# Gates by column reduction and a DRAM round trip instead of a row accumulation and ones products, with a fourth transpose bank

## The chip, the core and the metric

The kernel runs on one core of a Trainium2 chip. The metric is device time in microseconds from start to end of one execution. Five engines run their own instruction streams: TensorE (PE, whose weight loads the profile lists as PEld), VectorE (DVE), ScalarE (ACT), GpSimd (POOL) and SyncE (SP, which here only issues transfers). PSUM, the memory that PE writes, is used as eight tiles (banks) of 128 x 512 fp32.

## What is computed

A decoder trunk of two layers over 256 tokens of width 1024. Each layer is a feed-forward half step, a token mixer (block attention in the first layer, latent attention in the second) and another feed-forward half step. Every sub-layer has a shift, a scale and a gate computed from the conditioning vector `c`:

```
c_act = silu(c)
for layer in range(2):
    mods = c_act @ ada_w[layer] + ada_b[layer]
    sh1, sc1, g1, sh2, sc2, g2, sh3, sc3, g3 = split(mods, 9)
    h = modulate(rms_norm(x, norm_g[layer, 0]), sh1, sc1)
    x = x + 0.5 * g1 * swiglu(h, w_gate, w_up, w_down)
    h = modulate(rms_norm(x, norm_g[layer, 1]), sh2, sc2)
    x = x + g2 * (moba_attention(h) if layer == 0 else mla_attention(h))
    h = modulate(rms_norm(x, norm_g[layer, 2]), sh3, sc3)
    x = x + 0.5 * g3 * swiglu(h, w_gate, w_up, w_down)
```

Each of the six gates is a vector of 1024, the product of `c_act` with a 1024 x 1024 matrix.

## The kernel before

Tokens lie in two tiles of 128 partitions. Weights come from DRAM through SP into three buffers `raw` (`wload`, L787), and `split` (L677 to L682) makes two parts of each 128 x 1024 piece: `hi` by a copy on ScalarE (L680), `lo` by a subtraction on DVE (L681). There are eight buffers of each. A product of near full precision is then three matmuls of such parts (`mm3`, L810 to L812), or two matmuls in the gate and up products of the feed-forward (L1017, L1025). Attention scores (L1097 in the first layer) and value products (L1152) use full fp32.

The modulation matrices stream in parallel, 512 KB a tile of 128 x 1024, through three buffers `adaw` (`ada_tile`, L705 to L708), and are worked off on DVE between the weights' subtractions. There are two ways:

- **Shift and scale** (`column`, L688 to L692). The matrix is stored transposed, so that a partition holds one output's row. One DVE instruction multiplies the tile by `c_b`, `silu(c)` in all partitions, sums along the row and adds the bias; a small instruction (`DVE_READ_ACCUMULATOR2`) writes the sum. The outcome is a column: one value a partition.
- **Gate** (`ada_gate`, L721 to L745). A gate multiplies values whose 1024 columns lie along the free axis (`resid`, L920), so it is needed as a row in all partitions. The matrix is stored untransposed; eight DVE instructions (L729) add tile times `c` into `acc` (128 x 1024, set to zero and given the bias row by GpSimd, L727 and L728). Then `acc` is split, and `sums` adds its 128 partitions by four matmuls with a matrix of ones, two to each half of 512 columns (L739, L740), in the tile `adaps` of a PSUM bank kept for it (`ps_ada`). ScalarE copies the result, halved for feed-forward gates, into the gate tile (L742). There are two gate buffers.

The eight PSUM banks are four for products (`ps_mm`), three for transposes and attention (`ps_tr`) and that one.

The order of instructions on each engine is worked out on the host at build time by the class `Order`. It has each instruction's dependencies and an estimated length, and places instructions by need time on five engines, with buffers, banks and transfers in flight as limits (`place`). PE instructions of gate sums have a rule of their own: they are first in line (-1, L468 and L469) but are taken only after standing ready for `GATE_MARGIN` (L435), or when nothing else is there. After four rounds, `work_out` tries variations of the need times from the seeds in `TRIALS` and keeps each that ends earlier by its own estimate. Any change in the program therefore gives another order on every engine.

Of the kernel before, what the change touches and what calls it, by code (L numbers as in the profile page):

```python
# [22 lines left out]
P = 128  # L23
# [107 lines left out]
def lay_out(v):  # L131
# [13 lines left out]
    out["first"] = np.concatenate([first[:, :, :FIRST_A].reshape(KD, -1), first[:, :, FIRST_A:].reshape(KD, -1)], axis=1)  # L145
    mats, cols, rows = [], np.zeros((P, 3, NK), np.float32), []
    for key, i in vectors():
        w, b, c = ((v["kv_ada_w"], v["kv_ada_b"], i) if key == "kv" else
                   (v["ada_w"][key[0]], v["ada_b"][key[0]], 3 * key[1] + i))
        w, b = w[:, c * D:(c + 1) * D], b[c * D:(c + 1) * D]  # L150
        mats.append((w if i == 2 else w.T).reshape(KD, P, D))
        if i == 2:
            rows.append(b)
        else:
            c0 = NORMS.index(key) * KD
            cols[:, i, c0:c0 + KD] = b.reshape(KD, P).T
# [7 lines left out]
    for g in (v["mla_q_g"][0], v["mla_k_g"]):  # L164
        more += [np.concatenate([g[:DH], np.ones(P - DH, np.float32)])[:, None], np.tile(g[None, DH:], (P, 1))]
    out.update(ada=np.stack(mats), rows=np.stack(rows), cols=np.concatenate([cols.reshape(P, -1), *more], axis=1))

# [10 lines left out]
def bcast_row(ap, n, parts=P):  # L178
# [17 lines left out]
MARGIN = 400.0  # L196
GATE_MARGIN = 3000.0
ROUND_OF_ORDER = 4

TRIALS = (6, 9, 17, 64, 78, 124, 144, 157, 188, 238, 252, 394, 434, 436, 447, 579, 698, 701, 758, 764, 1127,  # L200
          1232, 1334, 1357, 1411, 1493, 1778, 1903)
ENGINES = ("PE", "DVE", "Activation", "Pool", "SP")
# [55 lines left out]
class Order:  # L258
# [128 lines left out]
    def place(self, need):  # L387
# [43 lines left out]
        def choose(e, t):  # L431
            av = avail[e]
            if e == "PE":
                first = min(av)
                old = [x for x in av if x[2] <= t - (GATE_MARGIN if x[0] < 0 else MARGIN)]  # L435
                x = min(old) if old else min(av, key=lambda x: (x[0] < 0, x))
                if x is not first and first[2] <= t and order[e] and order[e][-1] in self.pre[first[1]]:
                    x = first
                return x
# [16 lines left out]
        while placed < n:  # L456
# [9 lines left out]
            while known[e] and known[e][0][0] <= t:  # L466
                r, k = heapq.heappop(known[e])
                first = e == "PE" and any(u.startswith("adaps") for u in self.tiles_of[k])  # L468
                avail[e].append((-1 if first else need[k], k, r))  # L469
            x = choose(e, t)  # L470
# [104 lines left out]
def trunk(ctx: ExitStack, tc: tile.TileContext, a: dict, out: bass.AP):  # L575
# [10 lines left out]
    ps_mm = ctx.enter_context(tc.tile_pool(name="ps_mm", bufs=4, space=PSUM))  # L586
    ps_tr = ctx.enter_context(tc.tile_pool(name="ps_tr", bufs=3, space=PSUM))
    ps_ada = ctx.enter_context(tc.tile_pool(name="ps_ada", bufs=1, space=PSUM))

    uid = [0]  # L590

    def nm(s):
        uid[0] += 1
        return f"{s}_{uid[0]}"
# [57 lines left out]
    make_identity(nc, ident)  # L652
    ones_r = cp.tile([P, P], F32R, name="ones_r")
    ones = ones_r.bitcast(F32)
    nc.vector.memset(ones, 1.0)
    ident_b = cp.tile([P, P], BF16, name="ident_b")
# [14 lines left out]
    cols, cact = all_cols[:, :3 * NK].rearrange("p (i c) -> p i c", i=3), places["c"]  # L671
    m_cols = cp.tile([P, 2, NK], F32, name="m_cols")

    c_b = cp.tile([P, D], F32, name="c_b")
# [46 lines left out]
    def ada_gate(j, key, row):  # L721

        for k in range(KD):
            with noted(late if key == (1, 2) else set()):
                if k == 0:
                    acc = adap.tile([P, D], F32, tag="acc", name=nm("acc"), bufs=1)
                    nc.gpsimd.memset(acc, 0.0)  # L727
                    nc.gpsimd.dma_start(acc[0:1, :], a["rows"][row:row + 1, :])  # L728
                nc.vector.scalar_tensor_tensor(acc, ada_tile(j, k), cact[:, k:k + 1], acc, op0=ALU.mult, op1=ALU.add)  # L729
            if k < KD - 1:  # L730
                yield
        ahi, alo = split(acc, D)
        t = mods[key, "g"] = modp.tile([P, D], F32, tag="gate", name=nm("gate"))

        def sums():
            for hh in range(2):
                pt = ps_ada.tile([P, 512], F32, tag="ada", name=nm("adaps"))
                sl = slice(hh * 512, (hh + 1) * 512)
                nc.tensor.matmul(pt, ones_r, ahi[:, sl], start=True, stop=False)  # L739
                nc.tensor.matmul(pt, ones_r, alo[:, sl], start=False, stop=True)  # L740
                pe(0.44)
                nc.scalar.activation(t[:, sl], pt, AF.Copy, scale=1.0 if key[1] == 1 else 0.5)  # L742
            ready.add((key, "g"))
        later(3.0, sums)
        yield  # L745
# [72 lines left out]
    def tr_tile():  # L818
        return ps_tr.tile([P, 512], F32, tag="tr", name=nm("tr"))
# [747 lines left out]
    def first(units):  # L1567
# [5 lines left out]
        with ExitStack() as st:  # L1573
# [51 lines left out]
            hold(lambda: nc.scalar.activation(cact, cact, AF.Silu), 10e3)  # L1625
            ps_x = [tr_tile(), ps_ada.tile([P, 512], F32, tag="ada", name=nm("tr"))]
            accs = [tr_tile() if f >= 4 else mm_tile() for f in range(B1)]
# [119 lines left out]
```

## Time and profile before

| | |
|---|---|
| runs before | 991.25, 991.40 and 991.53 us; median 991.4 us |
| profiled execution | span 989.0 us from the first to the last instruction; its own whole time isn't listed apart, and the median of the runs is 2.4 us above its span |
| granted PE clock, mean | 0.996 |
| bytes read from and written to DRAM | 255.37 MB and 4.19 MB |

The profile has a page (busy time by engine, the chain of work that ended last, groups of equal instructions, transfers) and further views of the same trace: waits by who ended them, busy time in chosen windows, the instructions of one tile, and a timeline. In a row such as "L739 PE MATMUL adaps<-hi,ones_r 128*128 128x512 f32 x12 | 4.7, 394 | 0.0", L739 is the line of the kernel, then come engine, operation, what is written and read, shapes and how many; then busy us, mean ns of one, and idle time of the engine just before them with what ended it. Matmuls overlap in the pipeline, so their lengths add up to more than the time that they take.

The program's stages, by the profile's order of time: the first feed-forward until about 210 us, block attention until about 330, feed-forwards until about 515 and about 700, latent attention until about 800, and the last feed-forward.

### The profile page before, as it was taken

To read this page: it belongs to the slowest core of one execution; us is meant where nothing else is said; L and a number is where in the kernel's file an instruction comes from. 1 tells how busy PE (TensorE), PEld (TensorE's weight loads), DVE (VectorE), ACT (ScalarE), POOL (GpSimd) and SP (SyncE) were. 2 spreads that over 40 slices of the span, in tenths; PEclk is the share of its full clock that TensorE was granted. 3 is DMA by queue.
4 is the path that set the end of the run, shared out by engine and by line. 5 is a ranking of instruction groups with operands and counts; after the bars stand their busy time and mean duration, and the time that the engine had idled before them with its cause. 6 is when DMAs were issued, how large, how long until landed. Compare 5 with 4: busy or idle time off the path is not lost.

```text
span 989.0 us, 15277 instructions
## 1 busy us (share of the span) xinstructions
PE 978.4 (99%) x5583; PEld 832.5 (84%) x5583; DVE 845.8 (86%) x1433; ACT 631.5 (64%) x1180; POOL 83.8 (8%) x120
## 2 busy tenths in 40 slices
PE   8999999999999999999999999999999999999998
PEld 6988888878877888888888888888888888888887
DVE  7999999898998999999799999984899889677542
ACT  5689565378756966655367666643879796667421
POOL 1012010022230000000000000000142110000000
PEclk8999999999999999999999999999999999999999
DMA  9978989898777778988989988883343468545630
GB/s 368 408 253 286 338 301 360 307 346 316 261 291 232 246 281 321 334 317 300 366 294 344 339 308 310 291 301 109 107 155 119 179 233 302 191 171 173 229 131 22
DMA packets 53419, 260.57 MB, mean 263 GB/s; under 512 B 6208, under 2 KB 7008, under 8 KB 35168
## 3 DMA queue, kind: packets, MB, share of 16 engines
q1 hardware_dynamic: 51840, 255.93, 71.2%
q0 software_dynamic: 1024, 3.17, 1.1%
q8 instruction: 44, 0.72, 0.3%
q10 hardware_dynamic: 480, 0.49, 0.2%
q14 instruction: 31, 0.25, 0.1%
HBM read 255.37 MB, written 4.19 MB: 262 GB/s over the span
## 4 chain that ended last, share of the span: by engine, by line
PE 86%; issue 9%; DVE 3%; ACT 1%; POOL 1%; DMA 1%; SPq 0%; DVEq 0%; ACTq 0%; POOLq 0%
PE mm L1017 24%; PE mm L810 13%; PE mm L812 13%; PE mm L811 13%; PE mm L1025 12%; PE at L1152 1%; PE at L1132 1%; PE tr L1253 1%; PE at L1092 1%; PE tr L860 1%; PE tr L1524 1%; DVE lo L681 1%; PE at L1097 1%; PE mm L1694 1%; PE mm L1693 1%
## 5 line engine op out<-in xcount | busy, mean ns | idle before, releaser
L681 DVE TENSOR_TENSOR lo<-raw,hi 128x1024 fp32r<-128x1024 f32 (+3 forms) x312 | 369.4, 1199 | 66.7 <-ACT hi L680 61.3
L680 ACT ACTIVATE hi<-raw 128x1024 fp32r<-128x1024 f32 (+3 forms) x312 | 321.0, 1041 | 151.8 <-PE mm L812 114.5
L1017 PE MATMUL mm<-h,hi 128*128 128x512 f32 x1120 | 289.0, 394 | 0.0
L1017 PEld LDWEIGHTS mm<-h,hi 128*128 128x128 f32 x1120 | 199.6, 189 | 34.7 <-DVE g L955 0.3
L1025 PEld LDWEIGHTS mm<-h,lo 128*128 128x128 f32 x1120 | 155.7, 190 | 12.2
L1025 PE MATMUL mm<-h,lo 128*128 128x256 f32 x1120 | 162.5, 282 | 0.0
L691 DVE CUSTOM_DVE_ANT_0 adaw<-adaw,c_b,cols 128x1024 f32<-128x1024 f32 x112 | 142.0, 1280 | 3.7 <-ACT c_b L1624 1.9
L810 PE MATMUL mm<-hi,gh 128*128 128x512 f32 (+1 forms) x356 | 137.0, 388 | 0.0
L811 PE MATMUL mm<-lo,gh 128*128 128x512 f32 (+1 forms) x356 | 136.8, 387 | 0.0
L812 PE MATMUL mm<-hi,gl 128*128 128x512 f32 (+1 forms) x356 | 136.8, 387 | 0.0
L810 PE MATMUL mm<-hi,h 128*128 128x512 f32 (+1 forms) x240 | 93.7, 399 | 0.2
L811 PE MATMUL mm<-lo,h 128*128 128x512 f32 (+1 forms) x240 | 92.8, 392 | 0.0
L812 PE MATMUL mm<-hi,h 128*128 128x512 f32 (+1 forms) x240 | 91.9, 392 | 0.5 <-DVE h L826 0.4
L812 PEld LDWEIGHTS mm<-hi,gl 128*128 128x128 f32 x356 | 66.9, 188 | 13.6
L810 PEld LDWEIGHTS mm<-hi,gh 128*128 128x128 f32 x356 | 66.9, 188 | 13.4
L811 PEld LDWEIGHTS mm<-lo,gh 128*128 128x128 f32 x356 | 66.9, 188 | 13.2
L729 DVE SCALAR_TENSOR_TENSOR acc<-adaw,cols,acc 128x1024 f32<-128x1024 f32 x48 | 61.8, 1288 | 0.4 <-DMA adaw<-in_ada_dram 0.2
L810 PEld LDWEIGHTS mm<-hi,h 128*128 128x128 f32 x240 | 44.9, 188 | 10.0 <-issue 1.3
L812 PEld LDWEIGHTS mm<-hi,h 128*128 128x128 f32 x240 | 44.9, 188 | 9.7 <-DVE h L826 1.2
L811 PEld LDWEIGHTS mm<-lo,h 128*128 128x128 f32 x240 | 45.0, 188 | 7.9 <-issue 0.2
L954 ACT ACTIVATE u<-mm 128x256 f32<-128x256 f32 x70 | 26.4, 377 | 35.6 <-PE mm L1025 34.5
L847 POOL TENSOR_TENSOR rstd<-ssq,mhalf 128x1 f32<-128x1 f32 x12 | 13.7, 1139 | 411.3 <-DVE ssq L842 369.0
(241 smaller groups left out, 1257.3 us busy)
## 6 DMA issues: line engine op xcount, KB each, us to landing
raw<-in_w_dram SPq DMA_DIRECT2D x142, 1024.0 KB, 5.3
adaw<-in_ada_dram SPq DMA_DIRECT2D x160, 512.0 KB, 5.5
raw<-in_w_dram SPq DMA_DIRECT2D x12, 512.0 KB, 3.5
raw<-in_first_dram SPq DMA_DIRECT2D x7, 512.0 KB, 9.0
raw<-in_w_dram SPq DMA_DIRECT2D x6, 576.0 KB, 3.8
bias_d<-bt SPq DMA_DIRECT2D x12, 256.0 KB, 4.0
bg<-bias_d POOLq DMA_DIRECT2D x4, 768.0 KB, 7.7
raw<-in_first_dram SPq DMA_DIRECT2D x10, 256.0 KB, 8.7
```

The lines of the kernel that those rows point to most:

```text
L680: nc.scalar.activation(hi, src, AF.Copy)
L681: nc.vector.tensor_tensor(lo, src, hi.bitcast(F32), op=ALU.subtract)
L691: nc.vector.tensor_tensor_reduce(wt, wt, c_b, 1.0, cols[:, i, c:c + 1], op0=ALU.mult, op1=ALU.add, accum_out=m_cols[:, i, c:c + 1])
L729: nc.vector.scalar_tensor_tensor(acc, ada_tile(j, k), cact[:, k:k + 1], acc, op0=ALU.mult, op1=ALU.add)
L810: nc.tensor.matmul(ps, lh, rh, start=start, stop=False)
L811: nc.tensor.matmul(ps, lh, rl, start=False, stop=False)
L812: nc.tensor.matmul(ps, ll, rh, start=False, stop=stop)
L847: nc.gpsimd.tensor_tensor(r, stats[t], mhalf[:, 0:1], op=ALU.pow)
L860: nc.tensor.transpose(kslice(pt, j), kslice(y, j), ident)
L954: nc.scalar.activation(x, ps[:, S:], AF.Copy)
L1017: nc.tensor.matmul(ps[i], w[0], hs[2], start=k == 0, stop=False)
L1025: nc.tensor.matmul(ps[i][:, S:], w, hk_, start=False, stop=k == KD - 1)
```

## The change

- The gate's matrix is laid out transposed too, with output `8 p + k` in partition `p` of tile `k`, and the gate's eight tiles go through the same DVE instruction as shift and scale. The biases of all gates are one table `gates` of 128 x 48, loaded once into `g_cols`; each gate's eight columns there are its sums' starting values and are overwritten by the sums.
- For the four feed-forward gates a DVE instruction halves the eight columns.
- SP writes the 128 x 8 columns to a DRAM buffer of 1024 values, in which they stand as a row, and reads the row back into all 128 partitions as the gate tile.
- `acc`, its memset and bias load, its split, the matmuls with ones, the ScalarE copies, `ones_r` and the rule on gate sums in `Order` are gone. The bank of `ps_ada` goes to `ps_tr`, which has four. `TRIALS` has other seeds.

```
@@ lay_out
-        mats.append((w if i == 2 else w.T).reshape(KD, P, D))
+        mats.append(w.T.reshape(P, KD, D).transpose(1, 0, 2) if i == 2 else w.T.reshape(KD, P, D))
         if i == 2:
-            rows.append(b)
+            gates.append(b.reshape(P, KD))
...
@@ Order
-GATE_MARGIN = 3000.0
...
-                old = [x for x in av if x[2] <= t - (GATE_MARGIN if x[0] < 0 else MARGIN)]
-                x = min(old) if old else min(av, key=lambda x: (x[0] < 0, x))
+                old = [x for x in av if x[2] <= t - MARGIN]
+                x = min(old or av)
...
@@ trunk
-    ps_tr = ctx.enter_context(tc.tile_pool(name="ps_tr", bufs=3, space=PSUM))
-    ps_ada = ctx.enter_context(tc.tile_pool(name="ps_ada", bufs=1, space=PSUM))
+    ps_tr = ctx.enter_context(tc.tile_pool(name="ps_tr", bufs=4, space=PSUM))
...
+    g_cols = cp.tile([P, 6 * KD], F32, name="g_cols")
+    gate_d = [dp.tile([D], F32, name=f"gate_d{i}") for i in range(6)]
...
@@ ada_gate
+        if not row:
+            hold(lambda: nc.sync.dma_start(g_cols, a["gates"]))
+        g = g_cols[:, row * KD:(row + 1) * KD]
         for k in range(KD):
             with noted(late if key == (1, 2) else set()):
-                if k == 0:
-                    acc = adap.tile([P, D], F32, tag="acc", name=nm("acc"), bufs=1)
-                    nc.gpsimd.memset(acc, 0.0)
-                    nc.gpsimd.dma_start(acc[0:1, :], a["rows"][row:row + 1, :])
-                nc.vector.scalar_tensor_tensor(acc, ada_tile(j, k), cact[:, k:k + 1], acc, op0=ALU.mult, op1=ALU.add)
+                wt = ada_tile(j, k)
+                nc.vector.tensor_tensor_reduce(wt, wt, c_b, 1.0, g[:, k:k + 1], op0=ALU.mult, op1=ALU.add,
+                                               accum_out=g[:, k:k + 1])
...
-        ahi, alo = split(acc, D)
+        if key[1] != 1:
+            nc.vector.tensor_scalar(g, g, 0.5, None, op0=ALU.mult)
+        nc.sync.dma_start(gate_d[row].rearrange("(p k) -> p k", k=KD), g)
         t = mods[key, "g"] = modp.tile([P, D], F32, tag="gate", name=nm("gate"))
-
-        def sums():
-            for hh in range(2):
-                pt = ps_ada.tile([P, 512], F32, tag="ada", name=nm("adaps"))
-                sl = slice(hh * 512, (hh + 1) * 512)
-                nc.tensor.matmul(pt, ones_r, ahi[:, sl], start=True, stop=False)
-                nc.tensor.matmul(pt, ones_r, alo[:, sl], start=False, stop=True)
-                pe(0.44)
-                nc.scalar.activation(t[:, sl], pt, AF.Copy, scale=1.0 if key[1] == 1 else 0.5)
-            ready.add((key, "g"))
-        later(3.0, sums)
+        nc.sync.dma_start(t, bcast_row(gate_d[row], D))
+        ready.add((key, "g"))
         yield
```

Three places show how the order moves. The first is PE in block attention, at the scores of the last of four head groups. `at` and `mm` tiles written from `kT,qT` are scores (L1097 before, L1086 after); `mm` tiles written from `hi` or `lo` and `oT` are the output projection. Before:

```order
L1097 MATMUL at_3722<-kT_3691,qT_3690 128x128
L1097 MATMUL mm_3723<-kT_3691,qT_3690 128x128
L1097 MATMUL at_3724<-kT_3691,qT_3690 128x256
L810 MATMUL mm_3623<-hi_3494,oT 128x512
L811 MATMUL mm_3623<-lo_3495,oT 128x512
L812 MATMUL mm_3623<-hi_3494,oT 128x512
L810 MATMUL mm_3623<-hi_3494,oT 128x512
L811 MATMUL mm_3623<-lo_3495,oT 128x512
L810 MATMUL mm_3622<-hi_3650,oT 128x512
L1097 MATMUL at_3725<-kT_3691,qT_3690 128x256
L1097 MATMUL at_3724<-kT_3691,qT_3690 128x256
L1097 MATMUL at_3725<-kT_3691,qT_3690 128x256
```

After:

```order
L1086 MATMUL at_3700<-kT_3669,qT_3668 128x128
L1086 MATMUL mm_3701<-kT_3669,qT_3668 128x128
L1086 MATMUL at_3702<-kT_3669,qT_3668 128x256
L1086 MATMUL at_3703<-kT_3669,qT_3668 128x256
L1086 MATMUL at_3702<-kT_3669,qT_3668 128x256
L1086 MATMUL at_3703<-kT_3669,qT_3668 128x256
L799 MATMUL mm_3601<-hi_3472,oT 128x512
```

Before, six projection matmuls stand between the wide scores (128 x 256); after, the wide scores are one block.

The second is PE a little later, at the value products of the same group: `at` written from `pT,v` (L1152 before, L1141 after). Before:

```order
L1152 MATMUL at_3820<-pT_3804,v_3261 64x128 x2
L1152 MATMUL at_3820<-pT_3811,v_3261 64x128 x2
L810 MATMUL mm_3624<-hi_3785,oT 128x512
L811 MATMUL mm_3624<-lo_3786,oT 128x512
L812 MATMUL mm_3624<-hi_3785,oT 128x512
L811 MATMUL mm_3625<-lo_3629,oT 128x512
L810 MATMUL mm_3623<-hi_3650,oT 128x512
L1152 MATMUL at_3820<-pT_3818,v_3261 64x128 x2
L1152 MATMUL at_3820<-pT_3804,v_3261 64x128 x2
L1152 MATMUL at_3820<-pT_3811,v_3261 64x128 x2
L1152 MATMUL at_3820<-pT_3818,v_3261 64x128 x2
```

After:

```order
L799 MATMUL mm_3601<-hi_3628,oT 128x512
L1141 MATMUL at_3798<-pT_3782,v_3239 64x128 x2
L1141 MATMUL at_3798<-pT_3789,v_3239 64x128 x2
L1141 MATMUL at_3798<-pT_3796,v_3239 64x128 x2
L1141 MATMUL at_3798<-pT_3782,v_3239 64x128 x2
L1141 MATMUL at_3798<-pT_3789,v_3239 64x128 x2
L1141 MATMUL at_3798<-pT_3796,v_3239 64x128 x2
L801 MATMUL mm_3602<-hi_3763,oT 128x512
```

Five projection matmuls stood inside the block before, and none after. Counted over the whole program, blocks of full-precision matmuls (scores, value products and the few at the start) go from 25 to 22.

The third is SP at the third gate. `raw` rows load weights, `adaw` rows load modulation tiles. Before:

```order
L707 DMA adaw_4305<-in_ada_dram 128x1024
L787 DMA raw_4229<-in_w_dram 128x2048
L707 DMA adaw_4350<-in_ada_dram 128x1024
L707 DMA adaw_4384<-in_ada_dram 128x1024
L707 DMA adaw_4423<-in_ada_dram 128x1024
L787 DMA raw_4334<-in_w_dram 128x2048
```

After:

```order
L702 DMA adaw_4371<-in_ada_dram 128x1024
L730 DMA gate_d_103<-g_cols 128x8
L776 DMA raw_4204<-in_w_dram 128x2048
L702 DMA adaw_4393<-in_ada_dram 128x1024
L732 DMA gate_4252<-gate_d_103 128x1024
L702 DMA adaw_4440<-in_ada_dram 128x1024
L702 DMA adaw_4476<-in_ada_dram 128x1024
L776 DMA raw_4300<-in_w_dram 128x2048
```

The write of a gate's columns (L730) and the read of its row (L732) are new in SP's queue, here with two loads between them. At the first, second, fourth, fifth and sixth gate there are four, two, four, four and one.

More of the change, by code (lines that the diff above doesn't have):

```diff
@@ L145, in lay_out @@
     out["first"] = np.concatenate([first[:, :, :FIRST_A].reshape(KD, -1), first[:, :, FIRST_A:].reshape(KD, -1)], axis=1)
-    mats, cols, rows = [], np.zeros((P, 3, NK), np.float32), []
+    mats, cols, gates = [], np.zeros((P, 3, NK), np.float32), []
     for key, i in vectors():
@@ L165, in lay_out @@
         more += [np.concatenate([g[:DH], np.ones(P - DH, np.float32)])[:, None], np.tile(g[None, DH:], (P, 1))]
-    out.update(ada=np.stack(mats), rows=np.stack(rows), cols=np.concatenate([cols.reshape(P, -1), *more], axis=1))
+    out.update(ada=np.stack(mats), gates=np.concatenate(gates, axis=1), cols=np.concatenate([cols.reshape(P, -1), *more], axis=1))
     table = np.concatenate([np.zeros((1, H), np.float32), v["rel_bias"]])
@@ L196 @@
 MARGIN = 400.0
-GATE_MARGIN = 3000.0
 ROUND_OF_ORDER = 4
-TRIALS = (6, 9, 17, 64, 78, 124, 144, 157, 188, 238, 252, 394, 434, 436, 447, 579, 698, 701, 758, 764, 1127,
-          1232, 1334, 1357, 1411, 1493, 1778, 1903)
+TRIALS = (9, 33, 66, 73, 118, 140, 150, 394, 560, 798, 867, 1280, 1404, 1480, 1883, 2302, 3180, 3665)
 ENGINES = ("PE", "DVE", "Activation", "Pool", "SP")
@@ L467, in place @@
                 r, k = heapq.heappop(known[e])
-                first = e == "PE" and any(u.startswith("adaps") for u in self.tiles_of[k])
-                avail[e].append((-1 if first else need[k], k, r))
+                avail[e].append((need[k], k, r))
             x = choose(e, t)
@@ L652, in trunk @@
     make_identity(nc, ident)
-    ones_r = cp.tile([P, P], F32R, name="ones_r")
-    ones = ones_r.bitcast(F32)
-    nc.vector.memset(ones, 1.0)
     ident_b = cp.tile([P, P], BF16, name="ident_b")
@@ L1625, in first @@
             hold(lambda: nc.scalar.activation(cact, cact, AF.Silu), 10e3)
-            ps_x = [tr_tile(), ps_ada.tile([P, 512], F32, tag="ada", name=nm("tr"))]
+            ps_x = [tr_tile() for _ in range(2)]
             accs = [tr_tile() if f >= 4 else mm_tile() for f in range(B1)]
```

## The prediction

> **What bounds the kernel now.** I read the page's busy line and chain of waits first, then what TensorE (PE) waited for, then the windows.
>
> ```profile
> PE 978.4 (99%) x5583; PEld 832.5 (84%) x5583; DVE 845.8 (86%) x1433; ACT 631.5 (64%) x1180; POOL 83.8 (8%) x120
> ...
> PE 86%; issue 9%; DVE 3%; ACT 1%; POOL 1%; DMA 1%; SPq 0%; DVEq 0%; ACTq 0%; POOLq 0%
> ```
>
> The first line is busy time by engine, the second the share of the chain that ended last. PE carries both. Next, all that PE visibly waited for (total us, times, longest), three of seven rows:
>
> ```profile
> PE tr L1656 <- ACT diag L1646: 1.6, 2, 1.2
> ...
> PE mm L810 <- DVE qn L1544: 0.9, 2, 0.5
> ...
> PE tr L1524 <- ACT s L1117: 0.2, 1, 0.2
> ```
>
> The longest row is 1.6 us in 989.0, so no single wait is worth much. Windows, with busy time by engine in each stretch:
>
> ```profile
> 50.00:250.00 200.00, 199.86 (x1275) 168.64 (x1274) 186.84 (x344) 140.16 (x264) 28.26 (x53) 1.00 0.86 312
> 250.00:450.00 200.00, 199.96 (x1132) 167.81 (x1131) 187.12 (x316) 133.11 (x255) 19.83 (x14) 1.00 0.80 284
> 450.00:640.00 190.00, 190.00 (x991) 162.58 (x990) 177.30 (x262) 116.22 (x194) 3.00 (x2) 1.00 0.89 323
> ```
>
> Columns are start and end, length, then PE, weight loads, VectorE (DVE), ScalarE, GpSimd, granted clock, DMA share and GB/s. From 50 to 640 us PE has no gap, at granted clock 1.00; DVE is at 551.26 of 590, 93%. So an instruction taken off PE there shortens the kernel by its spacing, unless DVE, the next engine, holds it back.
>
> **The gate sums, removed.** The products with ones are two groups, and their surroundings in the last feed-forward read (start, length):
>
> ```profile
> L740 PE MATMUL adaps<-lo,ones_r 128*128 128x512 f32 x12 | 4.7, 395 | 0.0
> L739 PE MATMUL adaps<-hi,ones_r 128*128 128x512 f32 x12 | 4.7, 394 | 0.0
> ...
> 890.28 0.40 PE L739 MATMUL adaps<-hi,ones_r 128*128 128x512 f32 x1
> 890.51 0.39 PE L740 MATMUL adaps<-lo,ones_r 128*128 128x512 f32 x1
> 890.74 0.84 PE L1017 MATMUL mm<-h,hi 128*128 128x512 f32 x3
> ```
>
> A length of 0.40 overlaps the next matmul; what one costs the stream is start to start, 0.23 us (890.28, 890.51, 890.74), and none waits (0.0 idle). 24 matmuls x 0.23 = **5.5 us** off PE.
>
> **The extra transpose bank, as the new order uses it.** Full-precision attention matmuls (L1097 scores, L1152 values) stand in blocks among the others. Before, the last head group's scores are cut in two, since a score tile must wait for one of three banks; its last value products are cut too. After, both stand whole. The trace has both forms, whole first:
>
> ```profile
> 241.84 1.03 PE L1097 MATMUL at<-kT,qT 64*128 64x256 f32 x8
> 242.81 0.50 PE L810 MATMUL mm<-hi,h 128*128 128x512 f32 x1
> ...
> 304.41 0.59 PE L1097 MATMUL at<-kT,qT 64*128 64x256 f32 x2
> 304.94 0.50 PE L810 MATMUL mm<-hi,oT 128*128 128x512 f32 x1
> ...
> 306.20 0.40 PE L810 MATMUL mm<-hi,oT 128*128 128x512 f32 x1
> 306.53 1.13 PE L1097 MATMUL at<-kT,qT 64*128 64x256 f32 x6
> 307.58 0.50 PE L812 MATMUL mm<-hi,oT 128*128 128x512 f32 x1
> 307.92 0.39 PE L810 MATMUL mm<-hi,oT 128*128 128x512 f32 x1
> ```
>
> Eight wide score matmuls take 0.97 us whole (241.84 to 242.81), and 0.53 + 1.05 = 1.58 us cut (304.41 to 304.94, 306.53 to 307.58). The cut also adds one way in (306.20 to 306.53 is 0.33, against 0.23) and one way out (307.58 to 307.92 is 0.34), 0.1 each: 0.8 us in all. The value products, whole and cut:
>
> ```profile
> 302.35 1.58 PE L1152 MATMUL at<-pT,v 128*64 128x128 f32 x24
> 303.87 0.37 PE L1097 MATMUL at<-kT,qT 64*128 64x128 f32 x1
> ...
> 312.78 0.87 PE L1152 MATMUL at<-pT,v 128*64 128x128 f32 x8
> 313.57 0.50 PE L810 MATMUL mm<-hi,oT 128*128 128x512 f32 x1
> ...
> 314.93 1.30 PE L1152 MATMUL at<-pT,v 128*64 128x128 f32 x16
> 316.16 0.50 PE L812 MATMUL mm<-hi,oT 128*128 128x512 f32 x1
> ```
>
> Whole 1.52 us, cut 0.79 + 1.23 = 2.02, and 0.2 more for the way in and out: 0.7 us. Together **1.5 us**. The latent-attention layer has one block fewer in the new order as well; at one way in and out that is 0.2 us, left out of the sum. The rest of the rearrangement (new trial numbers, no delayed gate matmuls) I cost at nothing, between a gain of 2.9 us (rival one) and a loss of all of these 1.5 us.
>
> **DVE.** Gate products become the reduction that shift and scale already use:
>
> ```profile
> L691 DVE CUSTOM_DVE_ANT_0 adaw<-adaw,c_b,cols 128x1024 f32<-128x1024 f32 x112 | 142.0, 1280 | 3.7 <-ACT c_b L1624 1.9 <-DMA adaw<-in_ada_dram 1.7
> L729 DVE SCALAR_TENSOR_TENSOR acc<-adaw,cols,acc 128x1024 f32<-128x1024 f32 x48 | 61.8, 1288 | 0.4 <-DMA adaw<-in_ada_dram 0.2
> L691 DVE DVE_READ_ACCUMULATOR2_ANT m_cols<- 128x1 f32 x112 | 9.4, 84 | 0.0
> ...
> L681 DVE TENSOR_TENSOR lo<-acc,hi 128x1024 fp32r<-128x1024 f32 x6 | 7.3, 1220 | 1.1 <-ACT gh L825 1.1
> ...
> L1188 DVE TENSOR_SCALAR hv<-hv 128x8 f32<-128x8 f32 x8 | 1.4, 172 | 0.3
> ```
>
> Removed: 61.8 + 7.3 = 69.1 us. Added: 48 x (1.280 + 0.084) = 65.5, and four small scalings at 0.17 = 0.7: 66.2. DVE loses 2.9 us, 0.48 a gate. ScalarE loses 18 activations and GpSimd six memsets and six small loads; neither bounds a stretch. All of it is cover, so 0.
>
> **The round trip through DRAM.** Each gate now needs a write of 4 KB in pieces of 32 bytes, a wait on SP for its landing, and a 512 KB read of one row into all partitions; neither form is in the trace. Nearest rows (KB, median us to landing), from both sides:
>
> ```profile
> bias_d<-bt SPq DMA_DIRECT2D x12, 256.0 KB, 4.0
> bg<-bias_d POOLq DMA_DIRECT2D x4, 768.0 KB, 7.7
> ...
> out_dram<-x SPq DMA_DIRECT2D x2, 128.0 KB, 1.8
> ga_q<-in_mla_q_a_norm_g_dram ACTq DMA_DIRECT2D x1, 192.0 KB, 3.1
> ```
>
> Low 1.8 + 3.1 = 4.9 us, high 4.0 + 7.7 = 11.7. I take the high end, since small pieces give no reason for the low one. What hides it:
>
> ```profile
> 112.79 1.28 DVE L729 SCALAR_TENSOR_TENSOR acc<-adaw,cols,acc 128x1024 f32<-128x1024 f32 x1
> ...
> L920 DVE TENSOR_TENSOR ry<-mm,gate x25: 425/686/692, 181.5 to 985.1; 128x512 f32<-128x512 f32 x24, 128x256 f32<-128x256 f32 x1
> ```
>
> The first gate's products end within 5 us of the row at 112.79, its first use (L920) is at 181.5: over 60 us against 11.7. On the path it costs 0; uncovered, it would cost the whole 11.7 a gate. Of the extra load table, 24 KB behind the first weights, likewise 0. On SP, the read stands behind its write with one to four other transfers between them in the new order, and weight and modulation loads are queued behind it; that is the fourth rival.
>
> **Sum.** Span 989.0 - 5.5 - 1.5 = 982.0. The median of the runs, 991.4, lies 2.4 above the profiled span; I carry that over: **984.4 us**.
>
> **Rivals.**
>
> One: more of the hidden waiting goes. A wait below the overlap of two matmuls doesn't show as idle, but lengthens the mean:
>
> ```profile
> L810 PE MATMUL mm<-hi,gh 128*128 128x512 f32 x348 | 134.7, 390 | 0.0
> ...
> L810 PE MATMUL mm<-hi,h 128*128 128x512 f32 x224 | 88.0, 403 | 0.0
> ```
>
> The second group runs among transposes and attention, the first mostly without them: 13 ns x 224 = 2.9 us, giving 981.5. Against it: the only visible wait that a transpose bank could end is the row of 0.2 us. Chance 0.15.
>
> Two: DVE holds back part. Five of six gates fall in the stretch at 93%, where PE gains 5 x 4 x 0.23 = 4.6 and DVE only 5 x 0.48 = 2.4: if DVE sets the pace there, 2.2 us are lost, 986.6. For it: 93%. Against it: with PE busy all through these windows, DVE isn't late for it today. Chance 0.20.
>
> Three: the change frees PE of work, but PE was no limit, and the sums stood in slack; then only the 1.5 us remain, 989.9. For it: weight loads are at 84% in the busy line. The Trainium skill's page "Perfetto Trace Analysis", section "Identifying the Most-Contended Engine", says that matmul busy time is a poor measure of headroom and that weight-load busy time is a good one; by that rule PE has 16% to spare and this rival's time would follow. The trace disagrees where it can be tested: the starts at 890.28, 890.51 and 890.74 follow each other without slack. Chance 0.08.
>
> Four, slower: SP stops at the read until the write has landed, and the loads behind it come late. Three buffers of modulation tiles hold 3 x 1.36 = 4.1 us of DVE work. Were the write to take 7.7 us with nothing in between, 3.6 us a gate would go uncovered on DVE and then PE: six gates, 21.6 us, 1006. It outweighs the gain once more than 7.0 / 6 = 1.2 us a gate is uncovered, a landing of 5.3 us. Against it: the write row of 4.0, and the transfers between. Chance 0.05. The Trainium skill's page "DMA: Bandwidth & Descriptors", section "Anatomy of one DMA — SWDGE (gpsimd) path", gives about 2.0 us fixed for a DMA, mostly the receipt of the write, and warns that it can be long with HBM as target; by its figure alone, an estimate, this rival would cost nothing; the bias row of 4.0 is twice that.
>
> **The numbers.** Forecast 0.52, rivals 0.15, 0.20, 0.08, 0.05. Differences under 0.2% (2.0 us) can't be told from no change. Forecast and rivals one and two are faster by more: 0.87; rival three is within: 0.08; rival four slower: 0.05. The range reaches from just under rival one to rival two with the 1.5 us of the new order lost too (988.1): 981.0 to 988.5.
>
> **What would show it.** No matmul of gate sums, and 24 fewer in all; PE still without gaps from 50 to 640; in the last head group one block of eight wide score matmuls near 0.97 us and one of 24 value matmuls near 1.5; SP's wait at the gate read under 4 us, and none of PE, DVE or ScalarE waiting for the gate tile. Wrong would be PE waiting for low parts (L681) between 50 and 640, DVE waiting for modulation tiles, or the cut blocks back elsewhere.

## The result, and the profile after

| | before | changed |
|---|---|---|
| runs, median (lowest to highest) | 991.46 us (991.25 to 991.99), 4 runs | 982.65 us (982.59 to 983.01), 4 runs |
| profiled span | 989.0 us | 980.8 us |

The ratio is 0.9917, with a 95% interval of 0.9904 to 0.9929: 8.8 us faster. The forecast was 984.4, so 1.8 us more went than the sum of the prediction has. The forecast span was 982.0 and the measured one is 980.8: 1.2 of the 1.8 lie there. The rest is the 2.4 us that the prediction carried from span to whole time: the changed kernel's four runs lie 1.9 above their spans, and the 47 later runs of the kernel before 1.7 to 1.9 above theirs, so the profiled execution of before, at 989.0, was probably quicker than the median.

The size of the gain hangs on the runs of the kernel before, which spread more than those of the changed one: in the three sets beside the experiments they took 989.07 to 992.49 us, with medians of 990.95, 990.69 and 990.15. Against these the gain is 8.3, 8.0 and 7.5 us. The two profiled spans differ by 8.2.

The busy line of the changed kernel's page and the shares of its chain of waits (line numbers are now about 11 lower than before):

```profile
PE 969.2 (99%) x5556; PEld 826.1 (84%) x5559; DVE 834.1 (85%) x1478; ACT 612.2 (62%) x1162; POOL 74.6 (8%) x108
...
PE 86%; DVE 6%; DMA 3%; ACT 3%; issue 1%; POOL 1%; ACTq 0%; SPq 0%; DVEq 0%
```

PE is 9.2 us less busy and still fills 99% of the span. The same windows as before (PE, weight loads, VectorE, ScalarE, GpSimd, granted clock, DMA share, GB/s):

```profile
50.00:250.00 200.00, 199.93 (x1272) 168.75 (x1271) 186.24 (x359) 135.31 (x259) 23.25 (x49) 1.00 0.88 319
250.00:450.00 200.00, 199.91 (x1147) 168.92 (x1146) 191.56 (x348) 131.78 (x256) 17.10 (x9) 1.00 0.86 312
450.00:640.00 190.00, 189.70 (x981) 161.87 (x980) 175.41 (x268) 111.51 (x188) 2.99 (x2) 1.00 0.87 320
```

PE is idle for 0.46 of these 590 us (before: 0.18), and DVE is busy for 553.2 of them, 94%. What PE visibly waited for, over the whole span (total us, times, longest):

```profile
PE tr L1645 <- ACT diag L1635: 2.3, 2, 1.3
PE mm L1682 <- ACT h L814: 1.2, 1, 1.2
...
PE mm L800 <- DVE lo L676: 0.2, 1, 0.2
```

Low parts (L676) hold PE up once, for 0.2 us, at 699 us and so outside these windows. The new gate path: first the DVE groups (busy us, mean ns, idle before), then the instructions of the gate tile with who waited for it (nobody), the write's row, the transfers (KB, median us to landing) and SP's wait:

```profile
L724 DVE CUSTOM_DVE_ANT_0 adaw<-adaw,c_b,g_cols 128x1024 f32<-128x1024 f32 x48 | 60.9, 1276 | 0.0
L724 DVE DVE_READ_ACCUMULATOR2_ANT g_cols<- 128x1 f32 x48 | 3.8, 80 | 0.0
...
L909 DVE TENSOR_TENSOR ry<-mm,gate x25: 425/691/692, 179.6 to 976.8; 128x512 f32<-128x512 f32 x24, 128x256 f32<-128x256 f32 x1
L732 SPq DMA_DIRECT2D gate<-gate_d x6: 326/355/424, 127.1 to 833.6; - x6
...
who waited for it (us, times):
DMA to landing us min/median/max: 3.9/6.9/8.9
...
L730 SPq DMA_DIRECT2D gate_d<-g_cols x6: 326/355/425, 120.7 to 828.7; - x6
...
adaw<-in_ada_dram SPq DMA_DIRECT2D x160, 512.0 KB, 5.9
gate<-gate_d SPq DMA_DIRECT2D x6, 512.0 KB, 6.9
gate_d<-g_cols SPq DMA_DIRECT2D x6, 4.0 KB, 4.9
...
SPq L732 <- DMA gate_d<-g_cols: 5.0, 2, 3.4
```

The first write is issued at 120.7 us and the first read at 127.1. With the longest landing of a read, 8.9 us, the first gate stands at 136.0, and it is used at 179.6. SP stood before a read twice, for 5.0 us in all.

**Stage by stage.** The product with the gate tile (L920 before, L909 after) ends each sub-layer. The first such start in each cuts the span into stages: first feed-forward (A), block attention (B), two feed-forwards (C, D), latent attention (E), last feed-forward (F). Lengths in us, from the starts of these instructions in each trace; the kernels below the second row are those of the experiments:

| kernel | A | B | C | D | E | F |
|---|---|---|---|---|---|---|
| before | 181.5 | 137.9 | 164.3 | 186.0 | 120.2 | 164.5 |
| changed | 179.6 | 134.9 | 162.8 | 185.6 | 119.6 | 163.6 |
| e1 sums doubled | 181.9 | 138.4 | 166.1 | 187.0 | 120.2 | 165.4 |
| e7 written twice | 179.9 | 135.5 | 162.9 | 185.6 | 119.5 | 163.7 |
| e8 cuts put back | 180.1 | 137.5 | 162.8 | 185.6 | 119.5 | 163.5 |
| e2 sums, 4 banks, old seeds | 180.1 | 137.6 | 165.4 | 186.8 | 122.1 | 164.5 |
| e5 sums, 3 banks, no trials | 179.8 | 138.0 | 164.2 | 186.1 | 123.7 | 164.9 |
| e9 sums, 4 banks, no trials | 180.8 | 137.0 | 165.5 | 186.3 | 122.3 | 165.2 |
| e10 columns, 3 banks, no trials | 179.2 | 138.3 | 162.5 | 185.3 | 121.9 | 163.9 |
| e6 columns, 4 banks, no trials | 178.8 | 136.7 | 162.8 | 185.8 | 122.6 | 164.0 |
| e13 sums, 3 banks, searched on | 181.0 | 137.5 | 164.4 | 185.8 | 119.3 | 164.5 |
| e14 sums, 4 banks, searched | 182.4 | 134.6 | 166.8 | 186.3 | 120.1 | 164.5 |
| e11 columns, 3 banks, searched | 179.3 | 137.0 | 162.7 | 185.0 | 120.3 | 163.8 |
| e12 columns, 4 banks, other seeds | 181.8 | 135.0 | 162.8 | 185.7 | 120.1 | 163.7 |

Between the first two rows A lost 1.9, B 3.0, C 1.5, D 0.4, E 0.6 and F 0.9 us: 8.3 together, where the span lost 8.2. Of the six gates' sums, one gate's stood in A, one in B, two in C, one in D and one in F. At 4 x 0.23 = 0.9 a gate, B lost 2.1 us more than its sums, A 1.0 and E 0.6 more, C 0.3 and D 0.5 less, and F just them. These are single executions: the changed kernel and e7, which has its order on PE, differ by 0.3 in A and by 0.6 in B.

### The profile page after: what moved, and what is told of

It reads as the page before. It is cut to its first block, busy times and chain, and to the rows that moved or that the text cites. A ratio compares the mean times of both kernels' runs of the same rounds, so it can differ in the third digit from the quotient of the medians.

```text
span 980.8 us, 15216 instructions
## 1 busy us (share of the span) xinstructions
PE 969.2 (99%) x5556; PEld 826.1 (84%) x5559; DVE 834.1 (85%) x1478; ACT 612.2 (62%) x1162; POOL 74.6 (8%) x108
## 4 chain that ended last, share of the span: by engine, by line
PE 86%; DVE 6%; DMA 3%; ACT 3%; issue 1%; POOL 1%; ACTq 0%; SPq 0%; DVEq 0%
PE mm L1006 26%; PE mm L1014 14%; PE mm L799 13%; PE mm L800 13%; PE mm L801 13%; DMA raw<-in_first_dram 3%; DVE lo L676 1%; PE at L1121 1%; PE at L1141 1%; PE tr L1242 1%; ACT hi L675 1%; PE tr L849 1%; POOL rstd L836 1%; PE at L1086 1%; DMA cols<-in_cols_dram 1%
## 5 line engine op out<-in xcount | busy, mean ns | idle before, releaser
L676 DVE TENSOR_TENSOR lo<-raw,hi 128x1024 fp32r<-128x1024 f32 (+3 forms) x312 | 368.5, 1199 | 75.7 <-ACT hi L675 66.2
L1006 PE MATMUL mm<-h,hi 128*128 128x512 f32 x1120 | 282.9, 393 | 0.0
L1014 PEld LDWEIGHTS mm<-h,lo 128*128 128x128 f32 x1120 | 153.2, 190 | 10.7
L1014 PE MATMUL mm<-h,lo 128*128 128x256 f32 x1120 | 158.0, 283 | 0.0
L800 PE MATMUL mm<-lo,gh 128*128 128x512 f32 (+1 forms) x356 | 137.9, 387 | 0.0
L724 DVE CUSTOM_DVE_ANT_0 adaw<-adaw,c_b,g_cols 128x1024 f32<-128x1024 f32 x48 | 60.9, 1276 | 0.0
L836 POOL TENSOR_TENSOR rstd<-ssq,mhalf 128x1 f32<-128x1 f32 x12 | 15.8, 1315 | 540.3 <-DVE ssq L831 494.6
L943 ACT ACTIVATE g<-mm 128x256 f32<-128x256 f32 x70 | 26.2, 374 | 48.7 <-PE mm L1014 48.3
```

The lines of the kernel that those rows point to most:

```text
L676: nc.vector.tensor_tensor(lo, src, hi.bitcast(F32), op=ALU.subtract)
L724: nc.vector.tensor_tensor_reduce(wt, wt, c_b, 1.0, g[:, k:k + 1], op0=ALU.mult, op1=ALU.add, accum_out=g[:, k:k + 1])
L800: nc.tensor.matmul(ps, lh, rl, start=False, stop=False)
L836: nc.gpsimd.tensor_tensor(r, stats[t], mhalf[:, 0:1], op=ALU.pow)
L943: nc.scalar.activation(x, ps[:, S:], AF.Copy)
L1006: nc.tensor.matmul(ps[i], w[0], hs[2], start=k == 0, stop=False)
```

## The experiments

The theory was that of the prediction: PE has no slack, so gate sums cost their spacing and cut blocks theirs. The rivals: sums stood in slack or DVE sets the pace; SP's new waits delay loads; the gain comes from the new order and not from the parts of the change. Each experiment has its own runs of the kernel before beside it: median 990.95 us for e1, e2, e7 and e8, 990.69 for e5, e6, e9 and e10, 990.15 for the rest. The changed kernel itself was run in the first set alone (982.65).

**e1_sums_doubled: what is a matmul of the sums worth?** The kernel before, with its order kept and each sum given two more matmuls, with a matrix of zeros:

```
                 nc.tensor.matmul(pt, ones_r, ahi[:, sl], start=True, stop=False)
+                with noted(extra):
+                    for x in (ahi, alo):
+                        nc.tensor.matmul(pt, zeros_r, x[:, sl], start=False, stop=False)
                 nc.tensor.matmul(pt, ones_r, alo[:, sl], start=False, stop=True)
...
```

`noted(extra)` collects instructions that `Order` leaves out when it works out the order, so that all others keep their places.

> The kernel before, with 24 more matmuls: in each half of each gate's sums two products with a matrix of zeros are added in the same PSUM tile. The order of all other instructions is that of before, instruction for instruction. My theory (PE's stream is the limit and each such matmul costs its spacing): 24 x 0.23 = 5.5 us more than before, 997.0. Rival three (the sums stand in slack on PE): no change, 991.4 within 0.5. Rival two (DVE sets the pace between 50 and 640 us): only the last gate's four additions count, about 0.9 more, 992.3.

Measured: 995.52 us, ratio 1.0046 (1.0034 to 1.0059): 4.6 us slower, 3.4 to 5.8. The theory said 5.5 more, the rivals nothing and 0.9. One of the sums in the timeline of its PE (start, length):

```profile
899.04 0.39 PE L742 MATMUL adaps<-hi,ones_r 128*128 128x512 f32 x1
899.27 0.40 PE L745 MATMUL adaps<-hi,zeros_r 128*128 128x512 f32 x1
899.51 0.40 PE L745 MATMUL adaps<-lo,zeros_r 128*128 128x512 f32 x1
899.74 0.39 PE L746 MATMUL adaps<-lo,ones_r 128*128 128x512 f32 x1
899.98 1.12 PE L1031 MATMUL mm<-h,lo 128*128 128x256 f32 x8
```

The starts are 0.23 us apart here too. By the table of stages, C grew by 1.8 with its two gates, D by 1.0 and F by 0.9, and E, which has none, by 0.0. That is the full price of 0.9 a gate. Windows of e1 in C and in F:

```profile
330.00:505.00 175.00, 175.00 (x913) 149.74 (x912) 160.34 (x234) 103.18 (x174) 4.51 (x5) 1.00 0.84 305
800.00:985.00 185.00, 185.00 (x961) 158.33 (x960) 123.34 (x170) 104.07 (x178) 1.57 (x3) 1.00 0.53 192
```

PE is busy throughout in both, and the price is the same with DVE at 160.34 of 175 (92%) as at 123.34 of 185 (67%). A and B grew by 0.4 and 0.5, about half of it; one execution of each kernel can't tell that from the 0.3 and 0.6 by which the changed kernel and e7 differ there.

**e7_write_twice: do SP's waits cost anything?** The changed kernel, with its order kept and each gate's columns written twice. SP must let the first write land before the second, and the second before the read:

```
         nc.sync.dma_start(gate_d[row].rearrange("(p k) -> p k", k=KD), g)
+        with noted(extra):
+            nc.sync.dma_start(gate_d[row].rearrange("(p k) -> p k", k=KD), g)
...
```

> The changed kernel, with each gate's columns written to DRAM a second time before the row is read; all else in its order. SP must wait for the first write to land before it issues the second, and at two gates the read now stands directly behind the second write. My theory (the round trip and SP's waits are covered by the buffers): no change against the changed kernel, 982.7 within 0.5. Rival four (SP's wait at the landing makes loads late): with some 4 us for a landing and 1.2 us of it covered, 6 x 3 = 18 us more, 1000; half of that, 991, if only every second one bites.

Measured: 983.03 us (982.47 to 983.92), ratio 0.9921 (0.9909 to 0.9934), against 0.9917 (0.9904 to 0.9929) for the changed kernel. SP's waits at the second write (L733) and at the read (L735), and DVE's for modulation tiles, in the view of waits; the last row is from PE's timeline:

```profile
SPq L733 <- DMA gate_d<-g_cols: 15.3, 5, 4.4
SPq L735 <- DMA gate_d<-g_cols: 15.2, 5, 5.3
...
DVE adaw L687 <- DMA adaw<-in_ada_dram: 1.4, 1, 1.4
...
224.76 0.50 PE L803 MATMUL mm<-lo,h 128*128 128x512 f32 x1 [0.34 <-DVE lo L677]
```

SP stood for 30.5 us instead of 5.0, and the time didn't move by what these runs can tell. The longest stand was at the second gate, 3.3 and then 5.3 us, about 8.5 together, until 219.6. There the way of rival four shows, once and small: DVE waits 1.4 us for a modulation tile until 221.9, the low part that it makes next is late, and PE waits 0.34 us for it. Stage B is 0.6 us longer than in the changed kernel. At the other five gates SP stood for 2.7 to 5.7 us, and the loads behind it came in time for DVE.

**e8_cuts_back: what do the two cut blocks cost?** The changed kernel with its order kept but for two places on PE: six projection matmuls stand inside the last scores again, and five inside the last value products, as in the kernel before. `slow` marks the full-precision matmuls, `ends` holds the ends of their blocks, and `CUT` is 7:

```
-        for ks in self.work_out()[1].values():
+        for e, ks in self.work_out()[1].items():
+            if e == "PE":
...
+                ends = [j + 1 for j in range(len(ks) - 1) if slow[j] and not slow[j + 1]]
+                for end, tail, gap in ((ends[CUT], 3, 6), (ends[CUT + 1], 8, 5)):
+                    part = ks[end - tail:end + gap]
+                    ks[end - tail:end + gap] = part[tail:] + part[:tail]
```

> The changed kernel, with the two cuts of before put back in PE's order in the last head group (six projection matmuls inside the scores, five inside the value products); every other instruction in its place. My theory: the cuts cost 0.8 + 0.7 = 1.5 us, 984.2. Rival (the cuts only move work, and the pipeline hides the ways in and out): no change, 982.7 within 0.3. Rival (a cut also delays what follows, softmax and transposes): 3 us or more, 985.7.

Measured: 985.11 us (984.88 to 985.66), ratio 0.9942 (0.9928 to 0.9955): 2.1 us above e7 of the same set, 2.5 above the changed kernel. The theory said 1.5, the rivals nothing and 3 or more. The timeline of PE in the changed kernel, then in e8:

```profile
301.44 1.03 PE L1086 MATMUL at<-kT,qT 64*128 64x256 f32 x8
302.40 0.50 PE L799 MATMUL mm<-hi,oT 128*128 128x512 f32 x1
...
309.22 1.58 PE L1141 MATMUL at<-pT,v 128*64 128x128 f32 x24
310.73 0.50 PE L801 MATMUL mm<-hi,oT 128*128 128x512 f32 x1
```

```profile
302.00 0.59 PE L1094 MATMUL at<-kT,qT 64*128 64x256 f32 x2
302.53 0.50 PE L807 MATMUL mm<-hi,oT 128*128 128x512 f32 x1
...
304.12 1.13 PE L1094 MATMUL at<-kT,qT 64*128 64x256 f32 x6
305.17 0.50 PE L807 MATMUL mm<-hi,oT 128*128 128x512 f32 x1
...
311.02 0.87 PE L1149 MATMUL at<-pT,v 128*64 128x128 f32 x8
311.82 0.50 PE L809 MATMUL mm<-hi,oT 128*128 128x512 f32 x1
...
313.20 1.31 PE L1149 MATMUL at<-pT,v 128*64 128x128 f32 x16
314.44 0.50 PE L808 MATMUL mm<-lo,oT 128*128 128x512 f32 x1
315.19 0.50 PE L807 MATMUL mm<-hi,oT 128*128 128x512 f32 x1 [0.26 <-ACT oT L822]
```

Whole, the scores take 0.96 us (301.44 to 302.40) and the values 1.51; cut, 0.53 + 1.05 and 0.80 + 1.24. With the ways in and out that is the prediction's 0.8 + 0.7. New is the last row: behind the late values a projection waits for ScalarE's `oT`, and starts 0.75 us after the one before it, where 0.33 is usual (302.53 to the next at 302.86). That is 0.4 more, 1.9 in all; stage B is 2.0 longer than in e7, and no other stage by more than 0.2. The wait belongs to e8 and not to the kernel before, where the first projection behind the late values starts at 316.16 and the next one 0.34 us later:

```profile
316.50 0.39 PE L810 MATMUL mm<-hi,oT 128*128 128x512 f32 x1
```

So what the change took away by these two cuts is 1.5 to 1.6 us, e8's 2.0 without the 0.4.

**e2, e5, e6, e9, e10: gates and bank apart, and the search left out.** Any change of the program gives another order, and the two kernels have different trial seeds. So the two parts were taken singly, and in four kernels without any trials. e2 and e9 are the kernel before with its sums in the four shared banks; e10 is the changed kernel with three banks for transposes, the eighth bank being used at the start of A alone; e5 and e6 are the kernel before and the changed kernel. The edits of e9, then of e10 (e2 has e9's without the last pair of lines, e5 and e6 the last pair alone; left out is the line at the start of A that takes a tile of the eighth bank):

```
-    ps_tr = ctx.enter_context(tc.tile_pool(name="ps_tr", bufs=3, space=PSUM))
-    ps_ada = ctx.enter_context(tc.tile_pool(name="ps_ada", bufs=1, space=PSUM))
+    ps_tr = ctx.enter_context(tc.tile_pool(name="ps_tr", bufs=4, space=PSUM))
...
-                pt = ps_ada.tile([P, 512], F32, tag="ada", name=nm("adaps"))
+                pt = ps_tr.tile([P, 512], F32, tag="tr", name=nm("adaps"))
...
-TRIALS = (...)
+TRIALS = ()
```

```
-    ps_tr = ctx.enter_context(tc.tile_pool(name="ps_tr", bufs=4, space=PSUM))
+    ps_tr = ctx.enter_context(tc.tile_pool(name="ps_tr", bufs=3, space=PSUM))
+    ps_ada = ctx.enter_context(tc.tile_pool(name="ps_ada", bufs=1, space=PSUM))
...
-TRIALS = (...)
+TRIALS = ()
```

> The kernel before, its gates as before, but the sums' own bank joins the three transpose banks, which the sums now share; the order is worked out anew with the old trial numbers. In the new order the last head group's scores stand whole, its value products are cut in 4 and 8. My theory: the score cut goes, 0.8 us, and the new order adds or takes a microsecond: 990.6, between 989.5 and 991.6. Rival (the fourth bank is the larger part of the gain): 5 us or more gone, 986.5 or less. Rival (the bank does nothing, the sums now wait for banks): 991.4 or more.

> The kernel before with no trial numbers: the order is the best of the planner's four plain rounds. What the old trials are worth is its distance to before; my guess is 4 us, 995, since they removed waits of a few tenths at some thirty places. The four kernels of this set have no trials, so that bank and gates can be told apart without the search: this one has three transpose banks and gate sums.

> No trial numbers, four transpose banks that the gate sums share. My theory: the bank alone is worth 1.5 to 2 us, so that much under the untried kernel before; then the 2.3 us by which the four-bank kernel with the old trials was slower than before is the old trials' loss of effect on a program that they weren't chosen for. Rival (sums in the shared banks delay the transposes): no faster than the untried kernel before.

> No trial numbers, column gates, three transpose banks; the eighth bank is used in the first stage alone. My theory: 1.5 to 2 us over the untried changed kernel (the cuts are back), and 5.5 us under the untried kernel before. Rival (the bank is the larger part): within 3 us of the untried kernel before.

> The changed kernel with no trial numbers: four transpose banks, column gates. My theory (24 matmuls at 0.23, and bank and freed order about 2): 7 to 8 us under the untried kernel before, about 987. Rival (the gain beyond 5.5 us comes from luckier trial numbers): only 5.5 us or less under it.

Measured, without trials (ratio to the kernel before, interval):

| | 3 banks | 4 banks |
|---|---|---|
| sums | e5: 993.57 us, 1.0032 (1.0021 to 1.0044) | e9: 993.35 us, 1.0028 (1.0017 to 1.0040) |
| columns | e10: 987.71 us, 0.9973 (0.9962 to 0.9984) | e6: 987.30 us, 0.9969 (0.9957 to 0.9980) |

Down the columns, the gates are worth 5.9 and 6.1 us, near the 5.5 expected. Along the rows, the bank is worth 0.2 and 0.4, where 1.5 to 2 was expected; the two together are worth 6.3, where 7 to 8 was. e2, with the trial seeds of the kernel before, took 993.26 us, 1.0028 (1.0018 to 1.0039), outside the 989.5 to 991.6 expected: with another order under old seeds, the bank alone is slower than no change. The table of stages says where the bank's gain went. It shortens B by 1.0 with sums (e5 to e9) and by 1.6 with columns (e10 to e6). With sums A and C are then 1.0 and 1.3 longer and E 1.4 shorter; with columns C, D and E are 0.3, 0.5 and 0.7 longer. In A and C of e9 the sums of three gates take their tiles from the transposes' banks, which may be why; for e6 no such cause was found.

What the trials do shows in E. Without them it is longer: 123.7 in e5 against 120.2 and 119.3 in the kernel before and e13, 122.6 in e6 against 119.6 and 120.1 in the changed kernel and e12. PE's waits between 690 and 800 us, the two longest of seven in e5, then the longest of six in e6:

```profile
PE tr L1523 <- ACT v L1560: 1.1, 1, 1.1
PE tr L859 <- ACT y L854: 1.0, 1, 1.0
```

```profile
PE tr L1513 <- DVE kn L1548: 0.9, 1, 0.9
```

None of the three is among the waits of the kernel before or the changed kernel in that stretch.

**e11 to e14: the same, each with a search.** For each, seeds were tried in turn and those kept that end earlier by the estimate of `Order`: e11 is e10 with 26 trials, e12 the changed kernel with 36 others, e13 the kernel before with 16 trials added to its 28, e14 is e2 with 22 trials.

```
-TRIALS = ()
+TRIALS = (4, 6, 8, 27, 37, 53, 56, 63, 86, 91, 92, 97, 98, 108, 111, 115, 146, 181, 205, 227, 479, 1360, 1921, 3224, 3279, 3396)
```

These are the seeds of e11.

> Column gates with three transpose banks, and trial numbers found for this very program among seeds 0 to 3700, a span like that of the changed kernel's numbers. Its order has the last group's scores and value products cut again. Theory one (the fourth bank counts once the order is searched, since only then nothing else hides it): 1.5 to 2.5 us over the changed kernel, 984.2 to 985.2. Theory two (the bank is worth its 0.4 us of the untried pair, and the rest is the search): 983.1 within 0.7.

> The changed kernel with other trial numbers, found among seeds 9000 to 16000. If a search of this length gives its gain whatever the seeds, 982.7 within 1; if the changed kernel's numbers are a lucky draw, 984 to 987, on the way to the 987.3 of no trials.

> The kernel before with its own trial numbers and sixteen more, found by going on to seed 9000. Theory (the changed kernel's search merely went on longer, to seed 3665 against 1903): 988.5 or less. Theory (the search has less to find with the gate sums in PE's stream): 990 to 991, within 0.2% of before.

> Gate sums in four shared transpose banks, with trial numbers found for this program among seeds 0 to 3700; the last group's scores and values stand whole. Theory one (the bank counts once searched): 1.5 us or more under before, 989.3 or less. Theory two (the bank is worth little): 990 to 991.5. It also closes the square of bank and gates with a search each: the gates' part is its distance to the changed kernel, 6 us by the untried square.

| searched | 3 banks | 4 banks |
|---|---|---|
| sums | before: 990.15 us; e13: 989.68 us, 0.9995 (0.9986 to 1.0003) | e14: 990.98 us, 1.0010 (1.0001 to 1.0019) |
| columns | e11: 984.80 us, 0.9951 (0.9937 to 0.9965) | changed: 982.65 us, 0.9917 (0.9904 to 0.9929); e12: 985.93 us, 0.9961 (0.9948 to 0.9973) |

The gates' part is 5.4 us with three banks (before to e11) and, with four, 8.3 from e14 to the changed kernel or 5.1 from e14 to e12; 6 was expected.

The changed kernel and e12 differ in nothing but seeds, and by 3.3 us (3.1 by their spans; the changed kernel's runs are of another set). By the table of stages 2.2 of it lies in A. More than half of that is cut blocks again. Between 60 and 90 us the short transposes of the bias table (`tr` from `tab,oh`, 288 in both) stand among the matmuls in 16 blocks in the changed kernel and in 31 in e12. A matmul behind such a block takes longer from start to start, here 0.21 us (62.13 to 62.34) where the same matmul otherwise takes 0.12:

```profile
62.13 0.36 PE L1014 MATMUL mm<-h,lo 128*128 128x256 f32 x1
62.34 0.55 PE L1242 MATMUL tr<-tab,oh 128*128 128x64 bf16 x13
```

Summed over the matmuls behind these blocks, what they take beyond their usual spacing is 1.3 us in the changed kernel and 2.7 in e12. Stage B reads more plainly: the three searched kernels with four banks have 134.6, 134.9 and 135.0, the three with three banks 137.0, 137.5 and 137.9. e11 found the same cuts as the kernel before, in its timeline:

```profile
300.75 0.59 PE L1087 MATMUL at<-kT,qT 64*128 64x256 f32 x2
...
302.86 1.13 PE L1087 MATMUL at<-kT,qT 64*128 64x256 f32 x6
...
309.11 0.87 PE L1142 MATMUL at<-pT,v 128*64 128x128 f32 x8
...
311.26 1.31 PE L1142 MATMUL at<-pT,v 128*64 128x128 f32 x16
```

But the bank alone doesn't decide on the blocks. With three banks the scores are whole in e5 and the value products in e13; with four, the values are cut into 8 and 16 in e2, e6 and e9. The rows of e5, then of e13:

```profile
304.50 1.03 PE L1096 MATMUL at<-kT,qT 64*128 64x256 f32 x8
...
313.65 1.58 PE L1151 MATMUL at<-pT,v 128*64 128x128 f32 x24
```

Both blocks are whole only in the four-bank orders whose seeds were searched for them (the changed kernel, with e7 on its order, e12 and e14): there B is 134.6 to 135.5, and in every other kernel 136.7 to 138.4. So fourth bank and search together gave the whole blocks here, and in searched orders the bank is worth 2.0 to 2.1 us in B with columns (e11 against the changed kernel and e12). Whether the whole kernel keeps it depends on the draw: with the changed kernel's seeds it keeps 2.2 us, with e12's it is 1.1 slower than e11, and with sums (e14) nothing is left, since A and C are 1.4 and 2.4 longer than in e13.

## Why the prediction was right

- **The bound.** Right. PE still stands idle for only 0.46 us from 50 to 640, and e1 shows that 24 matmuls more cost 4.6 us (3.4 to 5.8) with the order kept.
- **The gate sums, 5.5 us.** Right in size: 5.9 and 6.1 without trials, 4.6 by doubling. The three enclose the forecast. In e1, C, D and F show the full price; A and B show half of it, and one execution can't tell whether part was hidden there.
- **Cut blocks, 1.5 us.** Right in place and size: the timeline of e8 has the 0.8 and the 0.7 as the prediction made them up; the other 0.4 in e8 are a wait that the kernel before doesn't have. The reason given, that a score tile must wait for one of three banks, isn't borne out as it stands: e5 has the scores whole with three banks, and three kernels with four banks have the value products cut. The prediction was safe from that because it read the blocks off the new order.
- **DVE, the DRAM round trip and the loads, 0.** Right. The gate groups take 64.7 us where 65.5 was worked out. DVE's busy line fell by 11.7 us, not 2.9; the gate's own groups make up 3.8 of that (69.1 less 60.9, 3.8 and 0.6), and no part of the forecast hangs on the rest. The two transfers land in 4.9 + 6.9 = 11.8 us by their medians, where 11.7 was taken; with SP's queue between them the first gate needed up to 15.3 (120.7 to 136.0), and had 58.9 (120.7 to 179.6).
- **The rest of the rearrangement, 0.** This is the step that was off. Of the 8.2 us of span, 4.6 to 6.1 are the gates and 1.5 to 1.6 the two cuts; the 0.5 to 2.1 that remain (1.2 by the forecast's own terms) are of the order. Stages A and E show them: 1.0 and 0.6 us beyond the sums. Of A's, 0.3 may be the dip of the clock told below, which the execution of before has as e7's does (0.66 from 10 to 20 us). Nothing in the change calls for it: e12, with the same change, has 2.2 us more in A. What the trials take off is 2.9, 3.9 and 2.4 us with sums (e5 to the kernel before of its set and to e13, e9 to e14) and 2.9, 1.4 and 4.7 with columns (e10 to e11, e6 to e12 and to the changed kernel). The changed kernel has the largest of the six, and as far as these runs show that is luck. The bounds given (2.9 and 1.5) held it, but the spread between two sets of seeds is 3.3 us, and no row of one profile could have told that.
- **The 2.4 us from span to whole time.** Too large by 0.5: 1.9 in the changed kernel's runs.
- **Rival one** (more of the hidden waiting goes) would have given 981.5, 1.2 below the outcome and so nearer than the forecast, but its mechanism didn't come. It would show as a lower mean of the first products; the two groups, in the changed kernel's view with shapes apart, are

```profile
L799 PE MATMUL mm<-hi,h 128*128 128x512 f32 x224 | 88.5, 402 | 0.0
L799 PE MATMUL mm<-hi,gh 128*128 128x512 f32 x348 | 135.4, 390 | 0.0
```

with 402 and 390 ns where it had 403 and 390 before. The waiting below the overlap is still there; the number came near by another way, by luck.
- **Rival two** (DVE holds back) falls: C and D, where DVE is busy, show the full price in e1, and between 50 and 640 us PE doesn't wait for low parts.
- **Rival three** (sums in slack) falls by e1 and by the four kernels without trials. It was the one that the Trainium skill's page "Perfetto Trace Analysis", section "Identifying the Most-Contended Engine", spoke for, by weight-load busy time as the measure of headroom. That stood at 84% before and after, and there was no headroom that these experiments could find.
- **Rival four** (SP's waits) falls in size by e7, and its point of decision was far too near. It took a landing of 5.3 us to be enough to eat the gain; in e7 SP stood for 2.7 to 8.5 us a gate, and only the longest of these reached DVE (1.4 us) and through it PE (0.34). In the changed kernel SP's longest wait at a read is 3.4 us, under the 4 that the prediction named as its sign, and DVE never waits for a modulation tile. The Trainium skill's page "DMA: Bandwidth & Descriptors", section "Anatomy of one DMA — SWDGE (gpsimd) path", with about 2.0 us fixed, was on the right side of that rival. Its figure is for transfers that GpSimd issues; here the 4 KB, issued by SP among the loads, landed after 4.9 us in the median, and after 2.5 at the least in e7.

What stays open: the rest of the 2.2 us between the two draws in A, and which places make up the 1.0 and 0.6 us that A and E lost beyond their sums.

## What to carry to other kernels

Where an engine has no gap, the start-to-start spacing of a group times its count is the price of that group, whatever its share of busy time says: here 24 x 0.23 = 5.5 us against 4.6 to 6.1 measured. Where two kinds of matmul alternate, count the changes between them too: here one cost about 0.1 us. Where a host program searches the order, a change can't be judged by one order of each kind: compare both without the search, and with two draws, and read the stages apart, since a gain in one stage can be lost in another without any cause in the change. A round trip through DRAM cost nothing here, where the time from its start to its first use (58.9 us at the first gate) was several times its landing time. The stand of the queue that issues it is a price of its own: of about 8.5 us of it at one gate in e7, 0.34 reached PE.

## What the runs showed of the hardware

The granted clock dips early in some profiled executions and not in others: in the window from 10 to 20 us it is 1.00 in the changed kernel and 0.66 in e7, which has the same order on PE. First the changed kernel, then e7:

```profile
10.00:20.00 10.00, 8.43 (x74) 8.23 (x75) 9.60 (x18) 7.12 (x15) 0.38 (x12) 1.00 1.03 407
```

```profile
10.00:20.00 10.00, 8.51 (x53) 8.21 (x54) 9.21 (x18) 6.34 (x13) 0.44 (x14) 0.66 1.03 409
```

PE got 21 matmuls less done in e7's window, but the first gate is used at 179.9 us against 179.6. The DMA engines are full there in both (share 1.03), so PE probably waits for loads there and can make it up; that wasn't tested. In these two executions the dip is worth 0.3 us. Of the changed kernel's four runs, the three with a mean clock of 1.000 took 982.59 to 982.67 us and the one with 0.996 took 983.01.

The small write was slow for its size: 4 KB in pieces of 32 bytes took 4.9 us to land, in the median, and a modulation tile of 512 KB, on the same queue, 5.9. Part of that is probably the loads ahead of it: in e7 the quickest second write, issued after SP had stood still, landed in 2.5 us.
